# A two-layer hybrid block: transfers planned by size, two slots moved between rings, and a margin on awaited results in the written order

## The chip, the cores and the metric

The kernel runs on one core of a Trainium2 chip. The metric is device microseconds of one execution; a time is the median of several. One core has five engines that run their own instruction streams: PE (TensorE, matrix products, with PEld for its weight loads), DVE (VectorE), ACT (ScalarE), POOL (GpSimd) and SP, which here only issues transfers. They meet through semaphores alone, so an engine that reaches an instruction whose input is not there stands still, and everything written behind it in its own stream stands with it.

## What is computed

Two layers of a post-norm block over 256 latent tokens and 256 context tokens of width 2048. Cut to what matters here:

```python
for l in range(2):
    mod_lat = silu(c) @ w_mod[l] + b_mod[l]              # 2048 x 6144, two vectors
    mod_ctx = silu(c_ctx) @ w_mod[l] + b_mod[l]
    h  = layernorm(x)   * (1 + scale)   + shift          # 256 latent rows
    hx = layernorm(ctx) * (1 + scale_x) + shift_x        # 256 context rows
    qa, ka, va, za, qb, kb, vb, zb, qkv_c, zc, ab = split(h @ w_in[l])     # the same for hx
    ya = softmax attention, 8 heads on 2 key/value heads, rms-normalised q/k, rotary, * silu(za)
    yb = neighbourhood attention, 4 heads, learned bias, * silu(zb)
    yc = gated delta scan, 4 heads, both directions, chunks of 64, rms-normalised, * silu(zc)
    y  = concat([ya, yb, yc]) @ w_out[l]
    x  = layernorm(alpha * x + gate * y)                 # ctx likewise, in layer 0 only
return x
```

All data is 32-bit floating point. The weights are read once, 288 MB in all, and nearly all the arithmetic is the two projections `w_in` and `w_out`.

## The kernel before

**Tiles.** A weight tile is 128 x 512 (256 KB). It is loaded raw, then split into a high part (a rounding copy, on ACT or DVE, function `high`) and a low part (raw minus high, always on DVE, `low_parts`); both parts bear the name `wHL`. A projection step is three matmuls on the tiles: high times high, high times low and low times high, into one PSUM accumulator (`acc` for `w_in`, `o` for `w_out`). The activations have the same two parts: `hH` and `hL` in layer 0, `hv` in layer 1 and in front of `w_out`. The modulation vectors are small products of `w_mod` tiles (`gvr`) with the two vectors `xs` (accumulator `md`, function `run_gv`); a part of the second layer's is computed on DVE from `gvl` tiles and a broadcast copy `xsb` of the vectors that is reloaded from DRAM every 256 columns (`mod_dve`).

**Staging.** One queue of weight tiles runs through the program: modulation, then layer 0's projections in the order of a table, heads in between, `w_out`, then layer 1. Heads (attention with `sc`, `P`, `ptr`, `PT`, `pv`, `otr`; delta scan with `scan`, `lv`, `S`, `O`, `vw`; scores' squares `qss`) are small chains that hop between PE, ACT and DVE. They have no loop of their own: their steps are put between the projection matmuls.

**What sets the order.** All instruction streams are written out by a planner that runs while the program is built (class `Order`, L104). It keeps a clock for each engine; every operation adds its cost to the clock of its engine (`op`, L119) after the planned ends of its inputs. Heads are generators; one that yields is continued by `poll` (L187), between two projection matmuls, as soon as PE's planned clock has reached its wait time, which `resume` (L164) sets: with a plain `yield` to the planned end of the results it made last. An instruction is thus placed on PE where, by the plan, its input is just ready; if the chip makes the result later than planned, PE stands. A `yield 0`, a wait for a ring's slot or for a flag, and the splits of weights (they are written by a hook, `split_ahead`) do not go by that rule. Transfers on SP have a planned issue time of 0.75 us and land 2.0 us after it, whatever their size and number (`Eng.call`, L370, which issues every instruction but PE's).

**Rings.** A `Ring` (L217) is a set of equal buffers, handed out when the planned clock has passed the release of one. The weights' ring `w` has 16 slots of 256 KB; at most 5 of them hold raw tiles (`RAWS`), and at most 3 tiles stand split ahead of use (`MOST`). The heads' ring `cin` has 15: the delta heads' convolved inputs, products and decay tables, gates and norm rows, and, in the first 130 us, modulation tiles.

Of the kernel before, what the change touches and what calls it, by code (L numbers as in the profile page):

```python
# [43 lines left out]
LAT_ONLY = ("qa", "za", "qb", "zb", "zc", "cq")  # L44

N_FIRST, LATE = 6, 3
LANDING = 1.5
ROPE_V = 0

# [54 lines left out]
class Order:  # L104
# [2 lines left out]

    LAT, DEP = 0.1, 0.13
    AHEAD, AHEAD_1 = 3.5, 2.5

    def __init__(self):
        self.t = {"PE": 0.0, "DVE": 0.0, "ACT": 0.0, "POOL": 0.0, "SP": 0.0}
        self.tasks, self.cur = [], None
        self.wr, self.rd, self.bank = {}, {}, {}
        self.hook = lambda: None
        self.ahead = self.AHEAD
        self.last = {}

    def op(self, eng, cost, outs=(), ins=(), lat=None):  # L119
        start = self.t[eng]  # L120
        if eng != "PE":
            start = max(start, self.t["PE"])
        bank = [r for a in list(ins) + list(outs) if a.space == PSUM for r in _regions(a)]
        ins = [r for a in ins for r in _regions(a)]
        outs = [r for a in outs for r in _regions(a)]
        for r in bank:
            for e, d in self.bank.get(r, {}).items():
                if e != eng:
                    start = max(start, d + self.LAT)
        for r in ins:  # L130
            e, d = self.wr.get(r, (eng, 0.0))
            if e != eng:
                start = max(start, d + self.LAT)
            elif eng != "PE":
                start = max(start, d + self.DEP)
        for r in outs:
            for tab in (self.wr, self.rd):
                e, d = tab.get(r, (eng, 0.0))
                if e != eng:
                    start = max(start, d + self.LAT)  # L140
        self.t[eng] = end = start + cost
        for r in bank:
            self.bank.setdefault(r, {})[eng] = end
        if lat is not None:
            eng, end = "dma", end + lat
        for r in ins:
            if self.rd.get(r, (eng, 0.0))[1] <= end:
                self.rd[r] = (eng, end)
        for r in outs:
            self.wr[r] = (eng, end)  # L150
        if self.cur is not None:
            self.cur.done[eng] = end + self.LAT
        self.last[eng] = end + self.LAT
# [10 lines left out]
    def resume(self, t):  # L164
        outer, last = self.cur, self.last
        self.cur, self.last = t, {}
        t.done = {}
        try:
            v = next(t.gen)
        except StopIteration:  # L170
            self.tasks.remove(t)
            v = None
        self.cur, self.last = outer, last
        if t not in self.tasks:
            return
        t.ring = None
        if isinstance(v, (Ring, Flag)):
            t.ring = v
            t.wait = self.t["PE"]
        elif isinstance(v, tuple):  # L180
            t.wait = v[1]
        elif v == 0:
            t.wait = self.t["PE"]
        else:
            t.wait = max(list(t.done.values()) + [self.t["PE"]]) + (v or 0.0)

    def poll(self):  # L187

# [155 lines left out]
class Eng:  # L344
# [19 lines left out]
    def __getattr__(self, f):  # L364
        fn = getattr(self.real, f)
        if f == "preload_act_table_set":
            return fn

        def call(*a, **k):
            r = fn(*a, **k)  # L370
            if f == "tensor_tensor_reduce":
                self.order.op(self.name, 0.4, [k["out"], k["accum_out"]], [k["in0"], k["in1"], k["scalar"]])
                return r
            ins = [x for x in list(a[1:]) + list(k.values()) if hasattr(x, "ap") and hasattr(x, "offset")]
            if f == "dma_start":
                self.order.op(self.name, 0.75 if self.name == "SP" else 1.0, a[:1], ins, lat=2.0)
            else:
                self.order.op(self.name, self.cost(f, a, k, ins), a[:1], ins)
            return r

        return call
# [23 lines left out]
def hybrid_grid_flow(  # L405
# [4 lines left out]
    od = Order()  # L410
# [6 lines left out]
    big = pool("big", bufs=1)  # L417
# [4 lines left out]
    hv = Slots(od, 32)  # L422
    spare = Spare(od, hv, range(16, 32))
    yq = Ring(od, big, "yq", 18)
    wr = Ring(od, big, "w", 16)
    tmp = Ring(od, big, "tmp", 5)
    P_r = Ring(od, big, "P", 3)
    cin = Ring(od, big, "cin", 15)
    mm, at, tr, cr, md = Ring(od, pp, "mm", 2), Ring(od, pp, "at", 2), Ring(od, pp, "tr", 1), Ring(od, pp, "c", 2), Ring(od, pp, "md", 1)

    def bc(ap, n):
# [20 lines left out]
    xs = const.tile([128, 2 * KT + 30], F32, name="xs")  # L452
# [275 lines left out]
    def run_gv(it):  # L728
        _, l, g, kt = it
# [14 lines left out]
        for j in range(4):  # L744
            c = j * w % 512
            T.matmul(
                ps[32 * j:32 * j + 32, 0:w], xs[:, 2 * kt:2 * kt + 32], ts[j * w // 512][:, c:c + w], cost=0.14 * w / 256,
                start=(kt == 0), stop=(kt == KT - 1), tile_position=(0, 32 * j),
            )
        for r in raw_ring.pop(it):  # L750
# [560 lines left out]
    def delta(l, h):  # L1311
# [182 lines left out]
            lv.append((yield from cr.get("lv"))[:, 0:256].rearrange("p (t c) -> p t c", t=4))  # L1494
        yield

        d_share = (0.7, 1.0)
        for lev, n in ((0, 32), (1, 64)):
            offs = [(0, n), (2 * n, 3 * n)] if lev == 0 else [(0, n)]
            od_ = [[(a, b) if d == 0 else (b, a) for a, b in offs] for d in range(2)]  # L1500
# [636 lines left out]
```

## Time and profile before

| | us |
|---|---|
| median of 3 runs (1694.78 to 1698.47) | 1696.52 |
| the profiled execution | 1699.39 |
| its span on the chip | 1697.6 |
| PE busy in it | 1634.8 (96%) |
| DVE busy | 1303.3 (77%) |
| ACT busy | 865.5 (51%) |

The times were taken on the device; the profile is of one execution, 2.9 us above the median. "Busy" counts an engine's own work and leaves out its waits and its issuing of transfers. Matmuls are pipelined: a 128 x 512 matmul is shown with some 400 ns, while the next begins after 227 ns, so "busy" on PE does not mean full rate. The profile also gives PE's granted clock for a stretch: 1.00 is 2.4 GHz, 0.5 is 1.2 GHz.

### The profile page before, as it was taken

Reading aid. Unit: us, or ns where it says so; the run is one execution under the profiler, and the core shown is the slowest. Engines: PE = TensorE matmul, PEld = TensorE weight load, DVE = VectorE, ACT = ScalarE, POOL = GpSimd, SP = SyncE. Lnnn points to the kernel's source line nnn. Section 1 sums busy time; section 2 is a strip of 40 time slices with the busy share of each in tenths; the row PEclk is TensorE's granted clock in tenths of the full one; section 3 lists DMA queues with packets and bytes.
Section 4 is the critical chain, followed back from the end, with each engine's and each line's share of the span. In section 5 each row is a group of like instructions: output and inputs, shape, how many; then the busy total and the mean of one; then the engine's idle time right before and its main releaser. Section 6 shows DMA issues by size and latency. Waiting matters only on the chain.

```text
span 1697.6 us, 30948 instructions
## 1 busy us (share of the span) xinstructions
PE 1634.8 (96%) x10527; PEld 1320.6 (78%) x10527; DVE 1303.3 (77%) x3943; ACT 865.5 (51%) x1969; POOL 43.1 (3%) x112
## 2 busy tenths in 40 slices
PE   4999999999999999999999999999999999999996
PEld 1657887787888778777788878778798888888875
DVE  4335788887888788878889798758688768687767
ACT  3234655463545344454644556654575655654543
POOL 0000100000001000000000000000000000000000
PEclk9999999999999999999999999999999999999998
DMA  9993544454455445444468796545454534344475
GB/s 321 350 350 120 156 132 137 147 160 146 148 178 167 149 156 178 139 129 138 130 200 259 257 301 204 168 120 157 126 163 125 160 95 155 118 130 148 151 232 182
DMA packets 213487, 296.33 MB, mean 175 GB/s; under 512 B 38384, under 2 KB 104656, under 8 KB 213328
## 3 DMA queue, kind: packets, MB, share of 16 engines
q1 hardware_dynamic: 211632, 291.07, 55.2%
q0 software_dynamic: 1696, 3.27, 0.7%
q8 instruction: 83, 1.36, 0.3%
q14 instruction: 76, 0.62, 0.1%
HBM read 287.88 MB, written 6.37 MB: 173 GB/s over the span
## 4 chain that ended last, share of the span: by engine, by line
PE 73%; DVE 12%; DMA 7%; ACT 4%; issue 3%; SPq 1%; DVEq 0%; ACTq 0%
PE acc L389 46%; PE o L389 11%; DMA gvr<-in_w_mod_dram 3%; DVE wHL L370 3%; PE md L389 3%; PE scan L389 3%; PE sc L389 2%; PE pv L389 2%; DMA raw<-in_w_out_dram 2%; DVE gvj L370 1%; PE ptr L399 1%; DVE gvl L370 1%; DMA raw<-in_w_in_dram 1%; DMA xsb<-xsd 1%; SPq L370 1%
## 5 line engine op out<-in xcount | busy, mean ns | idle before, releaser
L389 PE MATMUL acc<-hH,wHL 128*128 128x512 f32 x1664 | 576.4, 408 | 0.5 <-DVE hH L370 0.3
L370 DVE TENSOR_TENSOR wHL<-raw,wHL 128x512 fp32r<-128x512 f32 (+1 forms) x600 | 396.1, 671 | 77.3 <-ACT wHL L370 60.8
L389 PE MATMUL acc<-hv,wHL 128*128 128x256 f32 (+1 forms) x2496 | 441.3, 331 | 5.3 <-DVE wHL L370 3.5
L389 PEld LDWEIGHTS acc<-hv,wHL 128*128 128x128 f32 x2496 | 368.5, 191 | 57.2 <-issue 11.0
L370 ACT ACTIVATE wHL<-raw 128x512 fp32r<-128x512 f32 (+1 forms) x512 | 303.5, 611 | 200.6 <-PE o L389 52.8
L389 PEld LDWEIGHTS acc<-hH,wHL 128*128 128x128 f32 x1664 | 313.0, 188 | 85.5 <-issue 18.4
L389 PE MATMUL acc<-hL,wHL 128*128 128x512 f32 x832 | 325.5, 391 | 0.2 <-DVE hL L370 0.2
L389 PE MATMUL o<-wHL,hv 128*128 128x512 f32 x1092 | 256.0, 392 | 2.6 <-ACT hv L370 1.0
L389 PEld LDWEIGHTS o<-wHL,hv 128*128 128x128 f32 x1092 | 203.1, 188 | 49.7 <-DVE wHL L370 2.0
L389 PEld LDWEIGHTS acc<-hL,wHL 128*128 128x128 f32 x832 | 157.1, 189 | 30.8 <-issue 3.8
L370 DVE CUSTOM_DVE_ANT_0 gvl<-gvl,xsb,modT 128x256 f32<-128x256 f32 x224 | 108.2, 483 | 11.1 <-DMA xsb<-xsd 5.5
L370 DVE CUSTOM_DVE_ANT_0 gvj<-gvl,xsb,modT 128x256 f32<-128x256 f32 x224 | 107.4, 480 | 7.4 <-DMA xsb<-xsd 4.9
L389 PE MATMUL md<-gvr,xs 128*32 128x128 f32 (+1 forms) x1408 | 88.0, 349 | 25.6 <-DMA gvr<-in_w_mod_dram 24.9
L389 PEld LDWEIGHTS md<-gvr,xs 128*32 128x32 f32 x1408 | 32.7, 113 | 67.4 <-DMA gvr<-in_w_mod_dram 29.6
L370 ACT ACTIVATE P<-P,zz 128x512 f32<-128x512 f32 (+1 forms) x59 | 37.9, 655 | 66.1 <-DVE zz L370 65.0
L370 DVE TENSOR_TENSOR R<-R,Xt 128x60 f32<-128x60 f32 (+24 forms) x248 | 53.5, 216 | 9.1
L370 DVE TENSOR_TENSOR Xt<-X,R 128x60 f32<-128x60 f32 (+24 forms) x248 | 52.2, 211 | 7.9 <-ACT X L370 3.1
L370 DVE SCALAR_TENSOR_TENSOR cv<-acc,cw,cv 128x510 f32<-128x510 f32 (+1 forms) x48 | 33.8, 704 | 28.8 <-ACT cv L370 27.9
L389 PE MATMUL pv<-PT,v 128*128 128x128 f32 (+1 forms) x288 | 53.5, 302 | 2.3 <-ACT PT L370 2.3
L370 ACT ACTIVATE PT<-ptr 128x512 f32<-128x512 f32 (+1 forms) x57 | 33.7, 592 | 29.7 <-PE ptr L399 29.5
L370 ACT ACTIVATE hf<-htr,modT 128x256 f32<-128x256 f32 x62 | 31.6, 559 | 33.3 <-PE htr L399 33.1
L389 PEld LDWEIGHTS pv<-PT,v 128*128 128x128 f32 x288 | 43.1, 194 | 6.5 <-ACT PT L370 3.2
(302 smaller groups left out, 1869.3 us busy)
## 6 DMA issues: line engine op xcount, KB each, us to landing
raw<-in_w_in_dram SPq DMA_DIRECT2D x398, 256.0 KB
gvr<-in_w_mod_dram SPq DMA_DIRECT2D x256, 256.0 KB
raw<-in_w_out_dram SPq DMA_DIRECT2D x176, 256.0 KB
gvl<-in_w_modt_dram SPq DMA_DIRECT2D x256, 128.0 KB
raw<-in_w_in_dram SPq DMA_DIRECT2D x36, 128.0 KB
xp<-in_xin_dram SPq DMA_DIRECT2D x16, 256.0 KB
E<-growd SPq DMA_DIRECT2D x16, 256.0 KB
xres<-in_xin_dram SPq DMA_DIRECT2D x16, 256.0 KB
```

Of the source, the lines that this page charges most:

```text
L370: r = fn(*a, **k)
L389: r = self.real.matmul(out, lhsT, rhs, **k)
L399: r = self.real.transpose(out, in_, ident)
```

## The change

Five edits, all of them in what the planner counts; no instruction is added or taken away (15942 in both programs), and only their order on the engines and some choices of engine move.

1. Transfers: SP's planned issue falls from 0.75 to 0.37 us. A transfer lands at the later of two times: 2.0 us after its issue, as before, and 1.5 us (`DMA_TAIL`) after a new clock `dma`, to which every transfer adds its bytes at 390 KB per us (rows of 512 elements or more) or 349.
2. `MARGIN`: 0.25 us on the wait time after a plain `yield` or one with a number above zero.
3. The weights' ring has 14 slots instead of 16, the heads' ring 17 instead of 15.
4. A modulation matmul is planned at 0.10 us for 256 columns instead of 0.14.
5. The steps of the delta head's triangular solve (`lv`) are planned at 0.9 and 1.4 of a base instead of 0.7 and 1.0.

```diff
@@ class Order
+    MARGIN = 0.25
...
     def op(self, eng, cost, outs=(), ins=(), lat=None):
...
         if lat is not None:
-            eng, end = "dma", end + lat
+            n = 4.0
+            for x in outs_[0].shape:
+                n *= x
+            self.dma = max(self.dma, end) + n / (390e3 if outs_[0].ap[-1][1] >= 512 else 349e3)
+            eng, end = "dma", max(end + lat, self.dma + DMA_TAIL)
...
     def resume(self, t):
...
         else:
-            t.wait = max(list(t.done.values()) + [self.t["PE"]]) + (v or 0.0)
+            t.wait = max(list(t.done.values()) + [self.t["PE"]]) + (v or 0.0) + self.MARGIN
@@ Eng.call
-                self.order.op(self.name, 0.75 if self.name == "SP" else 1.0, a[:1], ins, lat=2.0)
+                self.order.op(self.name, 0.37 if self.name == "SP" else 1.0, a[:1], ins, lat=2.0)
@@ rings
-    wr = Ring(od, big, "w", 16)
+    wr = Ring(od, big, "w", 14)
-    cin = Ring(od, big, "cin", 15)
+    cin = Ring(od, big, "cin", 17)
@@ run_gv
-                ps[32 * j:32 * j + 32, 0:w], xs[:, 2 * kt:2 * kt + 32], ts[j * w // 512][:, c:c + w], cost=0.14 * w / 256,
+                ps[32 * j:32 * j + 32, 0:w], xs[:, 2 * kt:2 * kt + 32], ts[j * w // 512][:, c:c + w], cost=0.1 * w / 256,
@@ the delta head's triangular solve
-        d_share = (0.7, 1.0)
+        d_share = (0.9, 1.4)
```

What the edits move is seen in the written order. Three places, each before and then after; the names stand for the tiles above, "x4" for so many in a row.

**DVE, layer 1's attention heads, ahead of the high and low parts `HL` of a query tile `qa`**, which a score matmul `sc<-H,HL` on PE reads. `Xt` and `R` are steps of a delta head's triangular solve, `qt`, `rqs` and `qrt` norm and rotary steps of query tiles. Before:

```order
L370 TENSOR_SCALAR qt<-qt 128x2
L370 TENSOR_TENSOR rqs<-qr,qt 128x2
L370 TENSOR_TENSOR Xt<-X,R 128x66
L370 TENSOR_TENSOR R<-R,Xt 128x11x6
L370 TENSOR_TENSOR wHL<-raw,wHL 128x512
L370 TENSOR_TENSOR Xt<-X,R 128x60
L370 TENSOR_TENSOR R<-R,Xt 128x10x6
L370 TENSOR_TENSOR qrt<-qrt,rope 128x256
L370 TENSOR_TENSOR qa<-qa,qrt 128x256
L370 TENSOR_TENSOR wHL<-raw,wHL 128x512
L370 TENSOR_TENSOR HL<-qa,HL 128x256
```

After:

```order
L378 TENSOR_TENSOR Xt<-X,R 128x60
L378 TENSOR_TENSOR R<-R,Xt 128x10x6
L378 TENSOR_TENSOR Xt<-X,R 128x54
L378 TENSOR_TENSOR R<-R,Xt 128x9x6
L378 TENSOR_TENSOR wHL<-raw,wHL 128x512
L378 TENSOR_TENSOR Xt<-X,R 128x48
L378 TENSOR_TENSOR R<-R,Xt 128x8x6
L378 TENSOR_TENSOR wHL<-raw,wHL 128x512
L378 TENSOR_TENSOR HL<-qa,HL 128x256
```

The old piece begins behind the first score matmul `sc<-H,HL` as the program was written out, with ten instructions ahead of `HL`; in the new one the last four rows stand behind it, three instructions and `HL`. The norm and rotary steps have moved ahead of that matmul. On PE the rows here are nearly the same in both.

**PE, the end of layer 0's heads, up to its `w_out` matmuls** (`o`). Each `ptr` transposes probabilities into PSUM, ACT and DVE copy them out as `PT`, `pv` multiplies them with the values, `otr` transposes the result. Before:

```order
L389 MATMUL pv<-PT,v 128x128 x4
L399 MATMUL ptr<-cst,P 128x128 x4
L389 MATMUL acc<-hH,wHL 128x512
L389 MATMUL acc<-hL,wHL 128x512
L389 MATMUL acc<-hH,wHL 128x512
L389 MATMUL md<-gvr,xs 32x256 x4
L389 MATMUL pv<-PT,v 128x128 x4
L399 MATMUL ptr<-cst,P 128x128 x4
L399 MATMUL otr<-cst,o_9393 128x128 x4
L389 MATMUL pv<-PT,v 128x256 x2
L389 MATMUL o<-wHL,hv 128x512 x693
```

After:

```order
L397 MATMUL pv<-PT,v 128x128 x4
L407 MATMUL ptr<-cst,P 128x128 x4
L397 MATMUL acc<-hH,wHL 128x512
L397 MATMUL acc<-hL,wHL 128x512
L397 MATMUL acc<-hH,wHL 128x512 x2
L397 MATMUL acc<-hL,wHL 128x512
L397 MATMUL acc<-hH,wHL 128x512 x2
L397 MATMUL acc<-hL,wHL 128x512
L397 MATMUL acc<-hH,wHL 128x512
L397 MATMUL pv<-PT,v 128x256 x2
L397 MATMUL md<-gvr,xs 32x256 x4
L407 MATMUL otr<-cst,o_9068 128x128 x4
L397 MATMUL o<-wHL,hv 128x512 x699
```

The last `ptr` is followed by nine matmuls of `acc` instead of by `otr` at once, and one round of `pv` and `ptr` has moved further ahead.

**PE, the passage from layer 0 to layer 1**, where the new context rows (`res`) are transposed (`htr`) and become the activations of the context. Until then only matmuls of the latent rows (128x256) can run; those of 128x512 need the context too. Before:

```order
L389 MATMUL acc<-hv,wHL 128x256 x72
L389 MATMUL md<-gvr,xs 32x256 x4
L389 MATMUL acc<-hv,wHL 128x256 x18
L399 MATMUL htr<-cst,res 128x128 x8
L389 MATMUL acc<-hv,wHL 128x256 x9
L399 MATMUL htr<-cst,res 128x128 x4
L389 MATMUL acc<-hv,wHL 128x256 x18
L399 MATMUL htr<-cst,res 128x128 x4
L389 MATMUL ab<-hf,wab 32x256 x4
L389 MATMUL acc<-hv,wHL 128x256 x9
L399 MATMUL htr<-cst,res 128x128 x4
```

After:

```order
L397 MATMUL acc<-hv,wHL 128x256 x72
L397 MATMUL md<-gvr,xs 32x256 x4
L397 MATMUL acc<-hv,wHL 128x256 x72
L407 MATMUL htr<-cst,res 128x128 x12
L397 MATMUL acc<-hv,wHL 128x512 x6
L407 MATMUL htr<-cst,res 128x128 x4
L397 MATMUL ab<-hf,wab 32x256 x4
L397 MATMUL acc<-hv,wHL 128x512 x6
```

In the old order latent matmuls stand between the `htr` groups; in the new one all of them stand ahead, and behind the first twelve `htr` come matmuls of 128x512.

At the fourth place that the prediction speaks of, a scan of layer 0's first delta head, PE's stream has nine `acc` matmuls between `scan<-vw` and `scan<-S` in both orders, and in the new one two `pv` and four `ptr` beside them; DVE's reload `xsb` stands 57 instructions of the whole program ahead of the copies of `S` before and 90 after.

## Rows read from the trace of the kernel before

**Rows 1.** The page: busy time of each engine
```profile
PE 1634.8 (96%) x10527; PEld 1320.6 (78%) x10527; DVE 1303.3 (77%) x3943; ACT 865.5 (51%) x1969; POOL 43.1 (3%) x112
```

**Rows 2.** The page: PE's clock in 40 slices of 42 us
```profile
PEclk9999999999999999999999999999999999999998
```

**Rows 3.** Windows of the start: us, each engine busy (instructions), PEclk, DMA share, GB/s
```profile
0.00:50.00 50.00, 25.60 (x294) 11.43 (x295) 24.05 (x71) 16.11 (x31) 3.01 (x9) 1.00 1.00 323
```

**Rows 4.** Waits of PE after 150 us: us in total, times, longest us
```profile
PE acc L389 <- DVE wHL L370: 3.5, 4, 1.3
PE scan L389 <- DVE O L370: 3.4, 2, 2.8
PE sc L389 <- DVE HL L370: 2.7, 1, 2.7
PE pv L389 <- ACT PT L370: 2.3, 2, 2.0
PE qss L389 <- ACT P L370: 2.0, 1, 2.0
PE otr L399 <- DVE PTL L370: 1.5, 1, 1.5
PE otr L399 <- ACT PT L370: 0.7, 1, 0.7
...
PE gcum L389 <- DVE g_gg L370: 0.2, 1, 0.2
```

**Rows 5.** Timeline of PE around a scan: start us, us, instruction, [idle before, releaser]
```profile
311.30 1.16 PE L389 MATMUL scan<-S,cv 128*128 128x128 f32 x8 [2.80 <-DVE O L370]
```

**Rows 6.** Timeline of DVE, the same stretch
```profile
305.51 0.48 DVE L370 CUSTOM_DVE_ANT_0 gvj<-gvl,xsb,modT 128x256 f32<-128x256 f32 x1 [1.99 <-DMA xsb<-xsd]
```

**Rows 7.** Windows behind and around the long waits of PE, columns as above
```profile
311.30:315.00 3.70, 3.70 (x16) 3.16 (x17) 3.59 (x10) 2.16 (x4) 0.00 (x0) 0.70 0.09 32
1194.10:1201.00 6.90, 6.90 (x18) 5.41 (x19) 5.84 (x25) 2.84 (x8) 0.00 (x0) 0.55 0.11 38
1314.30:1320.00 5.70, 5.66 (x20) 4.57 (x21) 4.23 (x16) 3.01 (x7) 0.73 (x5) 0.70 0.29 63
843.00:849.50 6.50, 3.79 (x25) 3.03 (x18) 3.26 (x16) 5.38 (x13) 1.16 (x2) 0.74 0.53 96
```

**Rows 8.** Timeline of PE at the end of layer 0's heads
```profile
845.38 2.08 PE L389 MATMUL pv<-PT,v 128*128 128x128 f32 x8 [2.02 <-ACT PT L370]
849.00 0.66 PE L399 MATMUL otr<-cst,o 128*128 128x128 f32 x4 [0.69 <-ACT PT L370]
```

**Rows 9.** Timeline of DVE, layer 1: a solve step, a weight split, two rotary steps
```profile
1306.87 0.23 DVE L370 TENSOR_TENSOR R<-R,Xt 128x66 f32<-128x66 f32 x1
1308.12 0.68 DVE L370 TENSOR_TENSOR wHL<-raw,wHL 128x512 fp32r<-128x512 f32 x1
1311.32 0.41 DVE L370 TENSOR_TENSOR qrt<-qrt,rope 128x256 f32<-128x256 f32 x1
1311.77 0.42 DVE L370 TENSOR_TENSOR qa<-qa,qrt 128x256 f32<-128x256 f32 x1
```

**Rows 10.** Windows of the passage from layer 0 to layer 1
```profile
1066.00:1082.00 16.00, 13.05 (x109) 11.48 (x102) 15.83 (x36) 9.82 (x20) 0.00 (x0) 1.00 0.67 192
```

**Rows 11.** Timeline of PE in the passage
```profile
1077.96 0.64 PE L389 MATMUL md<-gvr,xs 128*32 128x256 f32 x8
1081.82 0.98 PE L399 MATMUL htr<-cst,res 128*128 128x128 f32 x7 [0.77 <-ACT res L370]
1082.56 1.32 PE L389 MATMUL acc<-hv,wHL 128*128 128x256 f32 x9
```

**Rows 12.** Tile raw: SP's issue, ns min/median/max
```profile
L370 SPq DMA_DIRECT2D raw<-in_w_in_dram x434: 327/333/1558, 32.5 to 1559.2; - x145
```

**Rows 13.** Chain of waits near the end: start us, us, what
```profile
1652.88 7.29 DMA raw<-in_w_out_dram
...
1674.20 10.77 PE o L389 x46
```

More of the change, by code (lines that the diff above doesn't have):

```diff
@@ L46 @@
 N_FIRST, LATE = 6, 3
+DMA_TAIL = 1.5
 LANDING = 1.5
@@ L115, in __init__ @@
         self.hook = lambda: None
+        self.dma = 0.0
         self.ahead = self.AHEAD
@@ L123, in op @@
         bank = [r for a in list(ins) + list(outs) if a.space == PSUM for r in _regions(a)]
+        outs_ = outs
         ins = [r for a in ins for r in _regions(a)]
```

## The prediction

> **What bounds the kernel now.** The first view is the page's busy time: PE works 1634.8 us of a span of 1697.6 [rows 1], so at most 62.8 us of waiting can go, whatever moves. The second is PE's clock by slices: full speed nearly throughout [rows 2]. The third is the start: in the first 50 us PE is busy for 25.6 with the transfers' share at 1.00 [rows 3], so 24.4 us of the 62.8 are there, and they hang on bytes. The order of loads on SP in that stretch is the same in both programs. The fourth is PE's waits after 150 us: 19 rows of releasers, 23.1 us in all, the first and the last of them shown [rows 4]. Five single waits make 10.2 of it: 2.8 for a scan, 2.7 for scores, 2.0 each for `pv` and `qss`, 0.7 for `otr` [rows 4, 5, 8]. The waits for weight splits make 5.1, of which the row shown has 3.5. What is left is 7.8 us in 16 places. The fifth view is the clock behind the long waits: 0.70 for 3.70 us after the scan's wait, 0.55 for 6.90 after the scores', 0.70 for 5.70 after `qss` [rows 7]. The loss is the missing share times the length: 1.1, 3.1 and 1.7 us. These stretches lie between levels because the clock came back to 2.4 GHz from 1.2 within them.
>
> So what the change can reach is about 23 us of waits and 6 of slow clock, 1.7% of the time. All of it arises where the planner took a result to be ready and the chip did not have it. My estimate for the bound below which it can't go is 1699.4 − 29 = 1670 on the profiled execution's time.
>
> **The change part by part.** I sum against the profiled execution, 1699.39 us; the median is 2.87 lower, and I take that off at the end.
>
> *The scan at 311.30.* PE waits 2.80 us for DVE [rows 5]; DVE itself had stood 1.99 us for the reload `xsb` just before [rows 6], so it reached the scan's copies late. In the new order the reload stands much earlier ahead of these copies, and two `pv` and four `ptr` more lie on PE in the gap. I expect 0.5 us to remain and the slow clock not to come: −2.3 − 1.1 = −3.4. If the reload lands as late as before: 0.
>
> *The scores at 1194.10.* PE waits 2.7 us for `HL` [rows 4]. Of the ten instructions that stood on DVE between the first score matmul and `HL`, seven are gone from there. Two rotary steps cost 0.41 and 0.42, a solve step 0.23, of which two fewer stand there, and a weight split 0.68, of which one fewer does [rows 9]: about 2.0 us, with two small norm steps that I put in at nothing. That leaves 0.7 of the wait. Whether the clock then falls is not shown by a wait of this size; I take 2.5 of the 3.1. Sum −2.0 − 2.5 = −4.5; the ends are 0 and −5.8.
>
> *The end of layer 0's heads at 845.* Waits of 2.02 and 0.69 [rows 8]. Before, three `acc` matmuls and four of `md` stand between `ptr` and the `pv` that needs it, now nine `acc`. At 0.234 us for a 128x512 matmul (46 in 10.77 [rows 13]) nine are 2.1 us; three and an `md` group were 0.7 and 0.6 (its four matmuls show as eight records, 0.64 us [rows 11]). The cover grows by 0.8 us, and one round of `pv` and `ptr` is gone from behind. I take −1.8, between −0.8 and −2.7. The clock of this stretch, 0.74 over 6.50 us [rows 7], holds the wait itself, so I add nothing for it.
>
> *`qss` at 1314.35.* 2.0 us and 1.7 of clock [rows 4, 7], behind a chain of copies that the order of after writes at other places. I see no reason for either outcome and take less than half: −1.5, between 0 and −3.7.
>
> *The margin on the rest.* 0.25 us covers at most 0.25 of each of the 16 places: 4.0 us. Some of them lie at the ends of the layers, where nothing is left to put between. I take −2.5, between −1 and −4.
>
> *Transfers and rings.* SP's issue takes 0.33 us [rows 12], so the new 0.37 is nearer than 0.75. The landing is not: a load on the chain near the end took 7.29 us [rows 13], while the planner now counts 256 KB as 0.67 + 1.5 us after its issue, or 2.0 if that is later; alone, a load is planned to be there 0.2 us sooner than before, and only in a burst later. A split written too early stops DVE or ACT, not PE at once. The weights' ring loses two of 16 slots. Its caps allow five raw tiles and three split pairs ahead beside the pair in use, 5 + 6 + 2 = 13, so 14 is enough by count, with one spare instead of three. Bounds: 0 if the caps hold; if one split in each place of [rows 4] comes as late again, the 5.1 us double. I take +2.0, nearer to the count. The Trainium skill, page "DMA: Bandwidth & Descriptors", section "Anatomy of one DMA — SWDGE (gpsimd) path", gives some 2.0 us fixed and a bandwidth term of bytes over 436 GB/s; for 256 KB my estimate by that is 2.6 us. The row above has 7.29 and so disagrees under load; by the page the split waits would mostly vanish and the sum be some 7 us lower, by the row it stays.
>
> *Planned costs.* `md` at 0.10 and the solve at 0.9 and 1.4 alter no duration on the chip. In the start the `md` groups wait for bytes [rows 3], and fewer `acc` matmuls stand ahead of the last of them: 0, between −3 and +3. The ends of layer 1 and of the program hold nearly the same rows: 0, between −1.5 and +1.5.
>
> *The passage to layer 1.* Here the new order loses cover. Before, PE waits 0.77 us at `htr`, and between the groups of `htr` stand latent matmuls, nine in 1.32 us [rows 11]; now all are ahead of the first `htr`, and the 128x512 matmuls behind it need the context's parts, which ACT and DVE make only after `htr`. One such pass is a copy of ACT (0.6 us as for a split's half, an estimate from the 0.68 of DVE's [rows 9]) and two steps of DVE of that order, about 2 us uncovered once. But PE also arrives later at `htr`, so the 0.77 goes. I take +2.5, with the ends at 0 and +8 (rival below).
>
> *New waits.* The four long waits of before stood where plan and chip happened to differ, and the whole order is dealt anew with only 0.25 us more per step. I put in one such wait without its clock loss: +2.0 (between 0 and +6, two with the loss of [rows 7]).
>
> Sum: −3.4 − 4.5 − 1.8 − 1.5 − 2.5 + 2.0 + 0 + 2.5 + 2.0 = −7.2. 1699.39 − 7.2 = 1692.2 on the profiled execution; on the median 1696.52 − 7.2 = 1689.3.
>
> **The rivals.** A measurement of this kernel can tell about 0.2% from no change, 3.4 us: below 1693.1 counts as faster, above 1699.9 as slower.
>
> *The waits are dealt anew (same).* DVE is full in stretches (15.83 of 16.00 us in 1066 to 1082 [rows 10]); there a result is late by microseconds because of what is queued ahead of it, and 0.25 reaches none of that. Then the old long waits go (−11.2 with `qss`) and as many come elsewhere (+10), the margin gives 2.5, splits and passage cost 4.5: +0.8, about 1697. For it: the waits that I know are 2.0 to 2.8 us, ten margins long. Against it: two of the three pieces of order that I followed gained cover by much more than 0.25.
>
> *The passage runs dry (slower).* One mechanism, at 1065 to 1105. DVE bounds the passage [rows 10], so the plan's start of `htr` can be too early by some microseconds; with no latent matmul behind the first `htr`, PE then stands for the chain of each of the first pairs (two times 2 us), and falls to 1.2 GHz for a stretch like that after the scores (3.1 [rows 7]), with 1 us for the later groups: +8 instead of +2.5. Together with half of the named gains (−5.6 instead of −11.2) the sum is −7.2 + 5.5 + 5.6 = +3.9, about 1700.4; if the splits double as well, 1703.5. It decides from where PE stands over 6 us between the first `htr` and the end of the context's transposes.
>
> *All clear (faster by more).* If no new long wait comes, splits and passage cost nothing and the named places clear wholly, the sum is −7.2 − 6.5 − 3 = −16.7: 1680. A rule that would bring this about is the one above on a load's time; the trace so far doesn't bear it.
>
> *The change doesn't do what it says.* A margin moves a step by one matmul at most, 0.23 us, and where steps wait for a ring's slot, a flag or a `yield 0` it isn't added at all. Then 2.5 of the sum goes, and it is 1692: still faster by a hair, and counted half there and half with the same.
>
> **How the numbers follow.** My forecast as summed 0.44 (1684 to 1693); all clear 0.10; dealt anew, with half of the last rival, 0.25; the passage 0.21. Faster is 0.44 + 0.10 = 0.54, same 0.25, slower 0.21. The prediction is 1689.3. For 8 in 10 I leave out the lower half of all clear and something over half of the slower case's upper part: 1679 to 1702. The likeliest case's own range is 1684 to 1693.
>
> **What would show it.** In the profile of the changed kernel: the scan of the first delta head waits under 1 us for DVE and PE's clock is 1.00 behind it; the score matmul waits under 1 us for `HL`; the `pv` ahead of layer 0's `w_out` waits under 1.2 us for `PT`; the sum of PE's waits after 150 us falls from 23.1 to about 17; the waits for weight splits stay under 8. The first 150 us have the same idle time of PE within 3 us. I am wrong if that sum is at 23 or more, if the waits stand in new places of 2 us and more, or if PE stands over 6 us in the passage.

## The result and the profile after

The changed kernel takes 1711.82 us (median of 5, 1709.76 to 1713.24) against 1697.17 us of the kernel before (1694.78 to 1698.68): a ratio of 1.0087, 95% interval 1.0073 to 1.0100. It is slower by 14.65 us. The forecast was 7.2 us faster, and its range ended at 1702. The profiled execution has a span of 1711.1 us, 13.5 more than before.

The page of the changed kernel, busy time and PE's clock, against [rows 1, 2]:

```profile
PE 1638.9 (96%) x10527; PEld 1324.0 (77%) x10527; DVE 1302.0 (76%) x3938; ACT 876.5 (51%) x1974; POOL 42.4 (2%) x112
...
PEclk9999999999999999999999999999899999999998
```

The work is the same. What grew is the time in which PE stands, and the time that it runs slowly behind that. PE's waits after 150 us in the changed kernel (us in total, times, longest), against [rows 4]:

```profile
PE sc L397 <- DVE qv L378: 4.8, 2, 3.4
PE acc L397 <- DVE wHL L378: 4.7, 5, 2.1
PE css L397 <- ACT csq L378: 4.3, 1, 4.3
PE acc L397 <- ACT qrt L378: 2.3, 1, 2.3
PE o L397 <- ACT hv L378: 2.1, 2, 1.5
PE o L397 <- DVE gy L378: 1.9, 1, 1.9
```

All rows of this view sum to 32.8 us; before it was 23.1. The long waits of before (`scan`, `HL`, `pv`, `qss`) have gone or shrunk, and `qv`, `csq`, `qrt` and `gy` have come. By stretch, each the sum of such rows:

| PE's waits, us | before | after |
|---|---|---|
| 150 to 840 (layer 0) | 4.5 | 8.8 |
| 840 to 880 (end of its heads) | 3.0 | 0.2 |
| 880 to 1100 (`w_out`, passage) | 4.5 | 3.9 |
| 1100 to the last 115 us of PE (layer 1) | 7.8 | 13.9 |
| the last 115 us | 3.3 | 6.0 |

That is 9.7 us more. The missing share of the clock, summed over slices of 10 us from 150 to 1680, was 8.5 us and is 12.0. 9.7 + 3.5 = 13.2 of the 13.5 us. The first 150 us have 25.9 us without work of PE, 26.4 before.

**Layer 0: a reload.** PE, DVE and ACT of the changed kernel around 461 us, one timeline each (start, length, instruction, [idle before, releaser]):

```profile
467.18 1.87 PE L397 MATMUL css<-cst,csq 128*128 128x1 f32 x8 [4.28 <-ACT csq L378]
```

```profile
461.23 0.48 DVE L378 CUSTOM_DVE_ANT_0 gvj<-gvl,xsb,modT 128x256 f32<-128x256 f32 x1 [2.47 <-DMA xsb<-xsd]
...
462.89 0.48 DVE L378 CUSTOM_DVE_ANT_0 gvl<-gvl,xsb,modT 128x256 f32<-128x256 f32 x1 [1.18 <-DMA xsb<-xsd]
...
465.78 0.69 DVE L378 TENSOR_TENSOR cv<-cv,se 128x512 f32<-128x512 f32 x1
```

```profile
466.50 0.63 ACT L378 ACTIVATE csq<-cv 128x512 f32<-128x512 f32 x1 [4.94 <-DVE cv L378]
```

`cv` is a delta head's convolved input, `csq` its squares, `css` their sums on PE. DVE reaches the first products with `xsb` and stands 2.47 and 1.18 us for the two transfers of a reload; `cv` is written on DVE behind these products; ACT waits for `cv`, PE for ACT. It is the chain of [rows 5, 6] at another delta head.

**Layer 1: solve steps.** PE, DVE and ACT around 1200 us:

```profile
1195.15 0.96 PE L397 MATMUL acc<-hv,wHL 128*128 128x512 f32 x3 [2.27 <-ACT qrt L378]
...
1197.83 0.79 PE L397 MATMUL sc<-H,HL 128*128 128x512 f32 x1 [1.03 <-DVE HL L378]
...
1203.70 1.22 PE L397 MATMUL sc<-H,HL 128*128 128x512 f32 x2 [3.37 <-DVE qv L378]
```

```profile
1197.70 0.20 DVE L378 TENSOR_TENSOR Xt<-X,R 128x49 f32<-128x49 f32 x1
...
1200.81 0.78 DVE L378 COPY X<-R 32x256 f32<-32x256 f32 x2
...
1203.49 0.15 DVE L378 TENSOR_SCALAR qv<-qss 128x2 f32<-128x2 f32 x1
```

The wait for `HL` is there with 1.03 us (2.7 before [rows 4]), but one of 2.27 stands ahead of it and one of 3.37 behind: from 1197.70 to 1200.81 DVE does nothing but steps of the triangular solve, and `qv`, the norm of the next scores, comes after them.

**The end: `w_out` tiles.** PE and ACT of the changed kernel:

```profile
1650.51 22.97 PE L397 MATMUL o<-wHL,hv 128*128 128x512 f32 x93 [1.92 <-DVE gy L378]
```

```profile
1646.70 2.56 ACT L378 ACTIVATE wHL<-raw 128x512 fp32r<-128x512 f32 x4 [2.21 <-DMA raw<-in_w_out_dram]
```

ACT waits for a raw tile, DVE for ACT's high part, and `gy`, which empties the accumulator that PE needs, is queued on DVE behind the low part.

Behind the long waits PE's clock is low (us, each engine busy, PEclk, DMA share, GB/s), against [rows 7]:

```profile
467.10:474.40 7.30, 7.22 (x29) 6.66 (x30) 4.40 (x17) 4.47 (x19) 0.00 (x0) 0.57 0.34 118
1195.10:1205.50 10.40, 5.95 (x17) 4.18 (x18) 8.17 (x31) 4.19 (x9) 0.73 (x5) 0.59 0.20 39
...
1650.50:1656.00 5.50, 5.49 (x17) 4.38 (x18) 5.35 (x9) 1.78 (x3) 0.00 (x0) 0.69 0.31 102
```

Behind the 4.3 us at `css` the clock, mostly at 1.2 GHz, took another 0.43 x 7.30 = 3.1 us.

### The profile page after: what moved, and what is told of

Its sections match the earlier page's. It is cut to its first block, busy times and chain, and to the rows that moved or that the text cites. A ratio compares the mean times of both kernels' runs of the same rounds, so it can differ in the third digit from the quotient of the medians.

```text
span 1711.1 us, 31051 instructions
## 1 busy us (share of the span) xinstructions
PE 1638.9 (96%) x10527; PEld 1324.0 (77%) x10527; DVE 1302.0 (76%) x3938; ACT 876.5 (51%) x1974; POOL 42.4 (2%) x112
## 5 line engine op out<-in xcount | busy, mean ns | idle before, releaser
L378 ACT ACTIVATE wHL<-raw 128x512 fp32r<-128x512 f32 (+1 forms) x529 | 319.5, 614 | 276.8 <-PE acc L397 69.7
L397 PEld LDWEIGHTS acc<-hv,wHL 128*128 128x128 f32 x2496 | 367.4, 191 | 62.2 <-issue 10.2
L397 PEld LDWEIGHTS acc<-hH,wHL 128*128 128x128 f32 x1664 | 313.7, 189 | 87.7 <-issue 21.8
L378 DVE CUSTOM_DVE_ANT_0 gvj<-gvl,xsb,modT 128x256 f32<-128x256 f32 x224 | 107.2, 479 | 17.9 <-DMA xsb<-xsd 13.6
L397 PE MATMUL md<-gvr,xs 128*32 128x128 f32 (+1 forms) x1408 | 88.3, 352 | 24.3 <-DMA gvr<-in_w_mod_dram 23.1
L378 ACT ACTIVATE PT<-ptr 128x512 f32<-128x512 f32 (+1 forms) x55 | 32.6, 593 | 27.4 <-PE ptr L407 27.1
```

Of the source, the lines that this page charges most:

```text
L397: r = self.real.matmul(out, lhsT, rhs, **k)
```

## The experiments

Three theories were on the table. *Chains*: the margin lengthens the heads. *Reload*: transfers planned too short bring DVE to `xsb` too early. *Dealt anew*: any edit gives another order with its own long waits. A fourth was the forecast's rival of a short weights' ring. The table has the median, the ratio to the kernel before on the same chip with its interval (the runs come from several chips, on which the kernel before has 1696.2 to 1697.2 us), PE's waits after 150 us, DVE's waits for `xsb`, and PE's waits in its last 115 us.

| kernel | us | ratio | PE waits | `xsb` | last 115 us |
|---|---|---|---|---|---|
| before | 1697.2 | | 23.1 | 10.4 | 3.3 |
| changed | 1711.8 | 1.0087 [1.0073, 1.0100] | 32.8 | 17.3 | 6.0 |
| e1 changed, margin 0 | 1704.4 | 1.0038 [1.0028, 1.0048] | 26.0 | 11.3 | 7.1 |
| e2 margin alone | 1699.1 | 1.0014 [1.0004, 1.0024] | 26.0 | 5.2 | 4.0 |
| e3 rings alone | 1698.8 | 1.0010 [0.9998, 1.0022] | 22.1 | 8.4 | 5.1 |
| e4 transfers alone | 1708.7 | 1.0066 [1.0051, 1.0081] | 30.7 | 10.2 | 2.8 |
| e5 costs alone | 1694.0 | 0.9985 [0.9974, 0.9995] | 18.1 | 4.2 | 3.5 |
| e6 margin 0.02 alone | 1700.0 | 1.0017 [1.0003, 1.0030] | 24.2 | 2.4 | 1.0 |
| e7 changed, old transfers | 1708.1 | 1.0067 [1.0047, 1.0088] | 25.9 | 4.7 | 9.8 |
| e8 changed, old rings | 1706.4 | 1.0054 [1.0037, 1.0072] | 27.1 | 13.6 | 2.7 |
| e10 changed, no reloads | 1701.1 | 1.0024 [1.0011, 1.0037] | 24.9 | none | 6.3 |
| e10 before, no reloads | 1690.3 | 0.9955 [0.9939, 0.9972] | 18.7 | none | 3.0 |
| e11 transfers, no burst | 1694.0 | 0.9981 [0.9970, 0.9993] | 19.0 | 12.5 | 3.2 |
| e12 changed, `xsb` later | 1704.8 | 1.0046 [1.0032, 1.0060] | 28.0 | 6.5 | 6.2 |
| e13 changed, no solve | 1694.4 | 0.9986 [0.9977, 0.9996] | 21.8 | 15.0 | 6.4 |
| e13 before, no solve | 1686.1 | 0.9933 [0.9914, 0.9952] | 18.0 | 8.6 | 3.2 |
| e15 mended | 1713.0 | 1.0091 [1.0072, 1.0110] | 31.8 | 2.7 | 3.1 |
| e16 costs, `xsb`, rule | 1701.0 | 1.0020 [1.0009, 1.0031] | 22.2 | 6.2 | 3.5 |

### The margin: out of the changed kernel, and alone

```diff
-    MARGIN = 0.25
+    MARGIN = 0.0
```

> The changed kernel with the margin set to 0 and all else kept. Theory 'chains' (0.25 us on every step of a head lengthens its chain, so heads end late and the last part of each layer waits): the time comes back by 5 us or more, to 1707 or below. Theory 'reload' (the shorter planned issue of transfers makes DVE take up the reloads of xsb before they land): the margin isn't the cause, 1709 to 1714. Theory 'dealt anew' (every edit gives another order with its own long waits): anything from 1690 to 1715, and PE's long waits stand in other places than in either kernel.

```diff
+    MARGIN = 0.25
...
-            t.wait = max(list(t.done.values()) + [self.t["PE"]]) + (v or 0.0)
+            t.wait = max(list(t.done.values()) + [self.t["PE"]]) + (v or 0.0) + self.MARGIN
```

> The kernel before with the margin of 0.25 us alone. 'Chains': 1702 or more. 'Reload': 1692 to 1697, since the margin by itself only covers short waits. 'Dealt anew': 1685 to 1710, with the four long waits of before gone and others in their place.

Out of the changed kernel it gives 7.4 us back, alone it costs 2.3. *Chains* wanted 5 or more both times and has it once. *Reload* had the changed kernel at 1709 or more without the margin, and the margin alone at 1697 or less; neither came. The largest wait of e2, in PE's timeline of that kernel:

```profile
1299.81 4.69 PE L390 MATMUL acc<-hv,wHL 128*128 128x512 f32 x20
1312.35 2.09 PE L390 MATMUL acc<-hv,wHL 128*128 128x512 f32 x4 [7.84 <-ACT wHL L371]
```

It stands in neither kernel of the comparison.

### A margin that can cover nothing

```diff
-    MARGIN = 0.25
+    MARGIN = 0.02
```

(against e2.)

> The kernel before with a margin of 0.02 us alone, a tenth of one matmul, which by its meaning can cover nothing. If an edit works by its meaning: 1695 to 1698. 'Dealt anew': the places of PE's waits differ from before and the time is off by 2 us or more, to either side.

0.02 us on top of the kernel before costs 3.8 us by the medians, 2.9 by the ratio, with an interval of 0.5 to 5.1. PE at the end of layer 0's heads in this kernel:

```profile
849.14 0.71 PE L390 MATMUL scan<-rr,W 128*128 128x128 f32 x4 [2.16 <-DVE rr L371]
851.29 1.22 PE L390 MATMUL scan<-vw,E 128*128 128x128 f32 x4 [1.44 <-ACT vw L371]
858.54 1.35 PE L400 MATMUL otr<-cst,o 128*128 128x128 f32 x4 [6.03 <-ACT o L371]
```

The chain of a delta head ends after the last matmuls that could fill its gaps, so PE stands through it. This is *dealt anew* by itself: an edit without meaning moves a wait of 6.03 us into place. It also gives a measure for the other edits, though from one order only: some microseconds come from the order alone.

### Rings, costs and transfers alone

```diff
-    wr = Ring(od, big, "w", 16)
+    wr = Ring(od, big, "w", 14)
-    cin = Ring(od, big, "cin", 15)
+    cin = Ring(od, big, "cin", 17)
```

> The kernel before with 14 and 17 slots alone. If the weights' ring is short: 1702 or more, and PE's waits for weight splits rise from 5.1 us to 10 or more. 'Reload' and 'chains': 1695 to 1699. 'Dealt anew': 1685 to 1710 with waits for splits under 8 us.

```diff
-                ps[32 * j:32 * j + 32, 0:w], xs[:, 2 * kt:2 * kt + 32], ts[j * w // 512][:, c:c + w], cost=0.14 * w / 256,
+                ps[32 * j:32 * j + 32, 0:w], xs[:, 2 * kt:2 * kt + 32], ts[j * w // 512][:, c:c + w], cost=0.1 * w / 256,
...
-        d_share = (0.7, 1.0)
+        d_share = (0.9, 1.4)
```

> The kernel before with the two planned costs alone (modulation matmul 0.10, solve 0.9 and 1.4). If costs matter by their meaning: 1694 to 1698, hardly any move. 'Dealt anew': 1690 to 1708, with PE's waits of 1 us and more in other places than before.

The rings alone do not move the time beyond its interval, and waits for splits fall rather than rise (4.2 us, 5.1 before). The costs alone gain 2.2 us: the sum of the waits falls by 5.0 us. e5 is faster than both kernels.

```diff
-                self.order.op(self.name, 0.75 if self.name == "SP" else 1.0, a[:1], ins, lat=2.0)
+                self.order.op(self.name, 0.37 if self.name == "SP" else 1.0, a[:1], ins, lat=2.0)
...
-            eng, end = "dma", end + lat
+            eng, end = "dma", max(end + lat, self.dma + DMA_TAIL)
```

> The kernel before with the new planning of transfers alone (margin 0, old rings, old costs). 'Reload': DVE's waits for xsb rise from 10.4 us to 15 or more and the time to 1703 or more. 'Chains': 1695 to 1699. 'Dealt anew': 1685 to 1710, whatever the waits for xsb.

The time is what *reload* said, 11.9 us more; the reason isn't. DVE's waits for `xsb` are 10.2 us, as before. One wait makes the loss, shown by PE and by ACT of e4:

```profile
1282.84 4.23 PE L397 MATMUL acc<-hv,wHL 128*128 128x256 f32 x34
1301.24 1.31 PE L397 MATMUL acc<-hv,wHL 128*128 128x256 f32 x3 [14.18 <-ACT wHL L378]
```

```profile
1299.20 1.33 ACT L378 ACTIVATE X<-R 32x256 f32<-32x256 f32 x2 [15.09 <-DVE R L378]
1300.56 2.19 ACT L378 ACTIVATE wHL<-raw 128x512 fp32r<-128x512 f32 x4
```

In e4's order 62 solve steps stand in a row on DVE, where the kernel before has 24 at most; the copy of the solve's result is on ACT ahead of four weight splits, and PE gets no weights until the solve is done. In the code this can come from `until`, which resumes the task with the least wait time while it wants a buffer: the solve yields 0 after each step, so it is always the least, and all of it is written at once. The 7.84 us of e2 are the same picture: 60 solve steps in a row on DVE, and on ACT

```profile
1310.32 1.32 ACT L371 ACTIVATE X<-R 32x256 f32<-32x256 f32 x2 [15.10 <-DVE R L371]
1311.66 0.63 ACT L371 ACTIVATE wHL<-raw 128x512 fp32r<-128x512 f32 x1
```

So the margin and the transfers, two edits with nothing in common by their meaning, each brought such a row into place. The next kernel takes that away.

```diff
-            t = min(ready, key=lambda t: t.wait)
+            full = max(self.t["DVE"], self.t["ACT"]) > self.t["PE"] + self.ahead
+            t = min([t for t in ready if not (full and t.step)] or ready, key=lambda t: t.wait)
```

(`step` is set where a task yielded 0; the rest of e11 is e4.)

> The kernel with the new planning of transfers alone, and one rule more: where the planner must wait for a buffer, it doesn't write steps of the triangular solve while DVE or ACT is over 3.5 us ahead of PE, if anything else can go. If the 62 solve steps in a row made the 14.2 us wait: that wait goes, no more than 24 solve steps stand in a row, 1690 to 1697. If the new planning of transfers costs time by itself: 1703 or more. 'Dealt anew' adds some 4 us to either side.

1694.0 us: 14.7 less than e4, and 3 less than the kernel before. In its order no more than 16 solve steps stand in a row, and PE's longest wait of layer 1 is one of 2.9 us, in its waits after 1100 us:

```profile
PE acc L400 <- DVE Xt L381: 2.9, 1, 2.9
PE acc L400 <- ACT wHL L381: 1.5, 1, 1.5
```

So the new planning of transfers need not be slow; it had dealt a bad place. (The rule is an edit too, so part of the 14.7 can be a new dealing.) In the changed kernel, too, no more than 16 solve steps stand in a row, and this wait isn't among its causes. That the single edits add up to 14.0 us (2.3 + 2.0 + 11.9 − 2.2) is therefore chance.

### Old transfers, old rings

```diff
-            eng, end = "dma", max(end + lat, self.dma + DMA_TAIL)
+            eng, end = "dma", end + lat
```

(and 0.75 instead of 0.37.)

> The changed kernel with the old planning of transfers and all else kept. 'Reload': DVE's waits for xsb fall from 17.3 us to 8 or less, the 4.3 us wait at the second delta head goes, 1700 to 1705. 'Dealt anew': 1690 to 1712, and the rest of the waits isn't that of the changed kernel either. If the parts simply added up: 1711.8 less 11.9, 1700.

> The changed kernel with 16 and 15 slots again. If two weights' slots were missed: 1705 or less, and the waits for weight splits fall from 4.9 us. If the parts simply added up: 1709.8. 'Dealt anew': 1690 to 1715 with no relation to the splits.

Each gives some back, 3.8 and 5.5 us, of which the 3.8 is not clear of noise (1.0067 [1.0047, 1.0088] against 1.0087 [1.0073, 1.0100]); neither has the time that additive parts would give. *Reload* has its waits right in e7 (8 or less for `xsb`, 4.7 measured) and misses the time, 1700 to 1705. In e8 PE's waits for splits fall from 4.9 to 1.6 us, as two missed slots would have it, and the time is 1.4 us above the 1705 that went with that. Two columns of the table go by an edit's meaning all the same. DVE's waits for `xsb` are 2.4 to 10.4 us in the six orders with the old planning (before, e2, e3, e5, e6, e7) and 10.2 to 17.3 in the five with the new one and no other hand on it (changed, e1, e4, e8, e11). PE's waits in its last 115 us are 5.1 to 9.8 us in the seven runs with 14 slots for weights and 1.0 to 4.0 in the eleven with 16. These eighteen runs have fourteen orders between them (e10 and e13 below keep that of their kernel). In e7, 3.8 of its 9.8 are a late head; the seven agree without that too. The rows of e3's last stretch show where:

```profile
PE o L389 <- ACT hv L370: 2.3, 2, 1.3
PE o L389 <- DVE qb L370: 1.5, 1, 1.5
PE o L389 <- DVE gy L370: 1.1, 1, 1.1
```

### The reloads priced in an unchanged order

```diff
-                Q.dma_start(xb[:, r], rows.rearrange("(o a) b -> o (a b)", o=1).to_broadcast([128, 256]))
+                rows = rows.rearrange("(o a) b -> o (a b)", o=1).to_broadcast([128, 256])
+                if k0 == 0:
+                    nc.sync.dma_start(xr[:, r], rows)
+                od.op("SP", 0.37, [Stand(xr[:, r], k0)], [rows], lat=2.0)
```

(`Stand` gives the planner the regions that it had; the products on DVE, not shown, read `xr`, the copy of the first columns, throughout; 0.75 for the kernel before.)

> The changed kernel in exactly its own order on PE, DVE and ACT, with the reloads of xsb left out (the first columns' copy is used throughout, so the second layer's modulation is computed from the wrong columns; the planner still counts the reloads). It prices DVE's 17.3 us of waits for xsb. 'Reload': the wait of 4.3 us at css and the slow clock behind it (3.4 us in 460 to 480) go, 1702 to 1706. If DVE's waits are covered or another wait takes their place: 1710 to 1713.

> The kernel before in exactly its own order, with the same reloads left out (the second layer's modulation is wrong in the same way). 'Reload': the scan's wait of 2.8 us and the 1.1 us of slow clock behind it go, 1692 to 1694. If another wait takes their place: 1696 to 1698.

10.7 us go from the changed kernel and 6.7 from the one before, 0.9 and 1.7 us beyond the expected ranges, in the same order on PE, DVE and ACT. In the kernel before the scan of [rows 5] no longer waits at all. The place at `css` in e10 of the changed kernel, and its clock:

```profile
463.55 1.05 PE L402 MATMUL css<-cst,csq 128*128 128x1 f32 x8 [0.70 <-ACT csq L383]
```

```profile
463.50:470.80 7.30, 7.25 (x46) 6.55 (x47) 4.26 (x15) 4.78 (x19) 0.00 (x0) 1.00 0.35 111
```

4.28 became 0.70 and the clock is whole there (not over the whole kernel, see the last section). By the medians the reloads thus explain 4.0 us of the difference between the kernels, by the ratios 3.1; the three intervals together make this uncertain by about 4 us either way (an estimate, half-widths added as squares), so the times alone don't set it apart from nothing. PE's waits do: they fall by 7.9 us in the changed kernel and by 4.4 in the one before.

```diff
-            yield ("at", od.wr[raw_key(xb)][1] + LANDING)
+            yield ("at", od.wr[raw_key(xb)][1] + LANDING + 2.0)
```

> The changed kernel with the planner waiting 2 us longer for each reload of xsb. If edits worked by their meaning: DVE's waits for xsb fall from 17.3 us to 6 or less and the time to 1702 to 1706, as without the reloads. 'Dealt anew': the waits for xsb fall as well, but the time lies anywhere from 1690 to 1715, since the other waits change places too.

1704.8 us, and the waits for `xsb` fall to 6.5 (6 or less was expected), about as *reload* said. Layer 0 was dealt anew by it; layer 1's waits stand at the same instructions as in the changed kernel, 13.4 us.

### The solve priced in an unchanged order

```diff
-            V.tensor_tensor(
-                t, X[:, i + 1:32, i:i + 1].to_broadcast([128, r_, c_]), R[:, i:i + 1, 0:c_].to_broadcast([128, r_, c_]),
-                op=ALU.mult,
-            )
-            V.tensor_tensor(R[:, i + 1:32, 0:c_], R[:, i + 1:32, 0:c_], t, op=ALU.add)
+            two = [X[:, i + 1:32, i:i + 1].to_broadcast([128, r_, c_]), R[:, i:i + 1, 0:c_].to_broadcast([128, r_, c_])]
+            od.op("DVE", V.cost("tensor_tensor", [t] + two, {"op": ALU.mult}, two), [t], two)
+            two = [R[:, i + 1:32, 0:c_], t]
+            od.op("DVE", V.cost("tensor_tensor", two[:1] + two, {"op": ALU.add}, two), two[:1], two)
```

> The changed kernel in exactly its own order on PE, ACT and SP, with the 31 pairs of solve steps of each delta head left out on DVE (the planner still counts them; the solve's result is wrong). If queued solve steps hold up DVE ahead of the attention scores: the waits of 2.27, 1.03 and 3.37 us at 1195 to 1204 and that of 1.4 us for Xt go, PE's waits between 1100 us and the end part fall from 13.9 us to 7 or less, 1696 to 1703. If ACT or the weights make them: 12 us or more of them stay, 1708 or more.

> The kernel before in its own order with the same solve steps left out. The wait of 2.7 us for HL and its slow clock (3.1 us) go if solve steps make it: 1688 to 1692; if not, 1695 to 1698. If the solve is the cause of layer 1's difference, this gains less than the same edit on the changed kernel by some 5 us.

17.4 us go from the changed kernel and 11.0 from the one before; the times lie 1.6 and 1.9 us below the expected ranges. Layer 1's waits fall from 13.9 to 2.9 us and from 7.8 to 2.0. PE of the changed kernel without the solve, where 2.27, 1.03 and 3.37 us were:

```profile
1190.62 0.70 PE L397 MATMUL sc<-H,HL 128*128 128x512 f32 x2
1191.16 0.40 PE L397 MATMUL sc<-L,HL 128*128 128x512 f32 x1
1191.39 0.86 PE L397 MATMUL acc<-hv,wHL 128*128 128x512 f32 x3
1192.09 0.65 PE L397 MATMUL sc<-H,HL 128*128 128x512 f32 x2
```

So 6.4 us of the difference of 14.6 hang on solve steps that stand on DVE ahead of what PE needs; by the ratios it is 5.8, uncertain by about 4 us as above, so it is more than nothing and its size is open. PE's waits fall by 11.0 us in the changed kernel and by 5.1 in the one before. With the reloads' 7.9 against 4.4, that is 9.4 of the 9.7 us by which the waits of the two kernels differ, if the two prices may be added, which no run tried in the same order.

### The causes taken away together

e15 is the changed kernel with e8's rings, e12's line and e11's rule; e16 is e5 with 1.0 us in e12's line and the same rule.

> The changed kernel with 16 and 15 slots, 2 us more of planned waiting for xsb and the rule that keeps solve steps back while the planner waits for a buffer. If the named causes are the cause: DVE's waits for xsb 6 us or less, PE's waits of the last 115 us 4 us or less, 1692 to 1700. If only the dealing counts: 1690 to 1712.

> The kernel before with the two planned costs, 1 us more of planned waiting for xsb and the same rule for solve steps. It keeps what was seen to help and leaves out transfers, rings and margin: 1687 to 1696 if the causes are the named ones; up to 1702 if it is dealt badly.

In e15 the reloads and the end go as expected by themselves: 2.7 us of waits for `xsb`, 3.1 in the last 115 us. The time is 1713.0, above both ranges. PE at the end of layer 0's heads in e15:

```profile
848.20 0.61 PE L400 MATMUL scan<-vw,E 128*128 128x128 f32 x4
856.24 1.35 PE L410 MATMUL otr<-cst,o 128*128 128x128 f32 x4 [7.43 <-ACT o L381]
```

It is the late delta head of e6 again, 7.43 us, and layer 1 has 14.4 us of waits. e16 is 7 us slower than e5, within its range for a bad dealing only. Mending the causes that one order shows does not make the next order good. The fastest kernels with the whole work are e5 and e11, 1694.0 us each and both faster than before: e5 was found by no cause, and e11 by taking away a cause of e4 that neither kernel of the comparison has.

## Why the prediction was wrong

**What bounds the kernel: right.** Only waits and slow clock moved; 13.2 of 13.5 us are in these two sums. The first 150 us kept their idle time within 0.5 us, as forecast.

**The named waits: right, but worth little.** The scan of the first delta head no longer waits. The end of layer 0's heads waits 0.2 us instead of 3.0 (−1.8 was taken, −2.7 the end). `HL` has 1.03 us left, 0.7 was taken. `qss` is gone from the rows. The passage did not run dry. PE's two waits at the context's `htr` are 0.92 and 0.93 us; with one of 0.5 earlier, `htr` has 2.3 us instead of 0.8, but other waits of the stretch fell, and it has 3.9 us instead of 4.5, where +2.5 was taken:

```profile
1089.68 0.98 PE L407 MATMUL htr<-cst,res 128*128 128x128 f32 x7 [0.92 <-DVE res L378]
1091.59 0.63 PE L407 MATMUL htr<-cst,res 128*128 128x128 f32 x4 [0.93 <-DVE hf L378]
```

**New waits: the term that failed.** One new wait without clock loss, +2.0 with an end at +6, was put in. The named places and `qss` released about 9 us of waits; the sum nevertheless rose by 9.7, so that some 19 us of waits came new, and behind them the clock fell in four stretches. Of the slow clock that was taken off with the scan and the scores (−1.1 and −2.5) nothing came back in sum: 8.5 us became 12.0. The rival *dealt anew* had the mechanism and named the reason, that results are late by what is queued ahead of them on DVE. Its price was wrong: it let as many waits come as went. Nothing bounds the new ones by the old. e6 shows that 0.02 us may bring 6 in one place, and e4 shows 14 in one. (The case of *all clear* had −3 for the rest of the named places; by the prediction's own terms it is −4.9, which changes nothing here.)

**The score at 1194: the right wait, the wrong place to look.** The prediction followed DVE from the first score matmul to `HL`. The solve steps that no longer stood there stood just behind, ahead of the next scores' `qv` (3.37 us), and PE had already waited 2.27 us for ACT's `qrt` ahead of both. The wait moved by one step along the same queue. e13 shows it: without the solve all three go.

**Transfers: the step was seen half.** The prediction had it that a load alone is planned sooner than before, and then that a split written too early, ahead of its load, "stops DVE or ACT, not PE at once". The rows it quoted for the scan [rows 5, 6] showed the opposite, a reload that passed through DVE to PE with 2.80 us. That a shorter plan lengthens such waits (2 to 10 us in the orders with the old planning, 10 to 17 with the new) was not drawn. What the reloads cost, 10.7 us in the changed kernel against 6.7, is shown, with the scatter given above. By the case of *all clear* the waits for splits would have gone; they are 4.9 us, and ACT stood 2.21 us for a raw tile near the end. The Trainium skill, page "DMA: Bandwidth & Descriptors", section "Anatomy of one DMA — SWDGE (gpsimd) path", by whose figures a load of 256 KB lands in an estimated 2.6 us, speaks of transfers issued from GpSimd, while the weights here are loaded from SP; no run here tests its figure for a load that is alone.

**Rings: right by count, wrong at the end.** Waits for splits are 4.9 us, 5.1 before, so the +2.0 was not needed. But in the last 115 us, which were put at 0 ± 1.5, every order with 14 slots waits longer than every order with 16. That the edit of the rings does it is shown by these orders, alone (e3, 5.1 us against 3.3) and out of the changed kernel (e8, 2.7 against 6.0). Whether the two slots fewer for weights or the two more for the heads do it is not shown, since they moved together each time. The path through a late raw tile is only argued from the rows of ACT and DVE above: in the kernel before ACT stood longer for the raw tiles of `wHL` in PE's last 115 us, 4.9 us against 2.8, and PE waited less.

**The margin: not shown either way.** It may cover 0.25 us in each place. In e1, e2 and e6 its effect can't be told from the new dealing.

What stays open is by which step of the plan the changed kernel puts more solve steps in front of layer 1's scores. In the orders tried it takes two of the edits: without the margin (e1) PE waits 5.2 us in that stretch and with the old transfers (e7) 5.9, against 13.9; the rings don't decide it, e8 and e15 with 16 slots have 13.4 and 14.4. The changed kernel with the old planned costs was not run. The margin alone and the transfers alone have 12.2 and 21.1 there, of which 7.8 and 14.2 are the single waits shown above, which the changed kernel doesn't have.

## What to carry to other kernels

Where a planner writes out an order from its own clocks, a change to its numbers is a new order first and an improvement second: measure what an edit without meaning does (here 0.02 us: 3.8 us) before a gain of that size is put down to a cause. Following the long waits of the old profile into the new order tells which go and nothing of which come; the sum needs a term for those that is as large as what is there already. To price a cause, keep the order and take the work away, as with the reloads and the solve: then each wait that goes can be found at its instruction, where every edit of the plan gave a mixed answer. The difference of two such prices still has the scatter of four medians.

## What was not expected of the hardware

Two transfers of 128 KB for which DVE stood 3.65 us (2.47 + 1.18) cost PE 4.28 us of standing two engines further on, with 3.1 us of slow clock behind it. Leaving the reloads out gave 10.7 us, more than the 3.6 us by which that wait shrank and its clock loss together, since the smaller waits of layer 0 went with it: 8.8 us of waits there became 1.1.

The slow clock did not come back as a whole. In the profiled executions the span fell by 9.0 us, PE's waits by 7.9, and the missing share of the clock, summed as above, stayed: 12.0 us in the changed kernel, 11.9 without its reloads. The loss behind `css` was gone, but other stretches lost more, here in the changed kernel without the reloads:

```profile
1180.00:1190.00 10.00, 7.20 (x40) 6.07 (x39) 8.03 (x34) 3.88 (x10) 0.00 (x0) 0.83 0.52 167
1190.00:1200.00 10.00, 6.63 (x16) 4.65 (x16) 8.48 (x28) 6.25 (x16) 0.73 (x5) 0.50 0.15 25
...
1640.00:1650.00 10.00, 8.73 (x26) 6.99 (x27) 7.70 (x14) 2.45 (x5) 0.00 (x0) 0.66 0.48 140
```

From 1180 to 1210 that is 6.8 us, where the changed kernel has 5.2 with nearly the same waits, and from 1640 to 1660 3.4 instead of 1.7. In the kernel before it was the same: 8.5 us with the reloads, 8.6 without, though the scan's wait and the slow clock behind it had gone. So these runs show a wait's own length as its price; that the slow clock behind it comes back for the whole kernel too, as the prediction took it for the scan and the scores, they do not show. Without the solve it did fall, from 12.0 to 5.1 us.
